# Sums of FFN weight blocks in a fused decoder block: from subtractions on VectorE to accumulating DMAs

## The chip, the cores and the metric

The kernel runs on one core of a Trainium2 chip. The metric is the device time of one execution in microseconds (us). The engines are TensorE (PE; PEld is its weight load), VectorE (DVE), ScalarE (ACT), GpSimd (POOL) and SyncE (SP). DMAs are issued from the queues of SP and POOL here and run on the core's 16 DMA engines.

## The reference

One decoder layer over 512 tokens and 2048 channels in float32: two attention branches, gated and merged, and a SwiGLU FFN of width 5632. What the change touches is the FFN:

```python
x = x + gt1 * (merged @ w_out)
h2 = _rms(x, g_norm2) * (1 + sc2) + sh2
gate, up = jnp.split(h2 @ w_ffn_in, 2, axis=-1)
x = x + gt2 * ((jax.nn.silu(gate) * up) @ w_ffn_out)
```

## The kernel before

The first half of the span holds the adaLN products, the two attention branches, the merge and `w_out`. Its weights come through another pool of tiles and are not touched.

Both FFN products are made as seven products of 2x2 blocks in place of eight (Winograd's form of Strassen's scheme): P1, P5, P7, P3, P6, P2, P4, in this order. Each multiplies a block of activations, or a sum of such blocks, with a block of weights, or a sum of such blocks. `BLOCK` names the four blocks of a weight 11, 12, 21 and 22. P1, P3 and P2 take the blocks 11, 22 and 21 as they are; P5, P7, P6 and P4 take sums, which build on one another in place (`INTO`, line 1173).

The work is a list of pieces, one per product and quarter (`j`) of the contraction. In the first matrix (FFN-in, `ffn_in_group`, line 1243) there are 11 groups of four column tiles with 7 x 4 = 28 pieces each. In the second (FFN-out, `ffn_out_chunk`, line 1418) a piece is one group of the contraction; the groups stand in chunks (`CH`, line 1395) of 3, 2, 2, 2 and 2, each done for two halves `q` of the output: 154 pieces. A piece's raw weights are a 128x1024 float32 tile (512 KB), in rows of 1 KB, or of 512 bytes in the first group. `raw_load` issues the load on SP's queue into a pool of ten such tiles. `piece_make` subtracts two raw tiles on DVE where the product asks for a sum, then splits the tile: ACT casts it to a float32r upper part `whi`, DVE subtracts that from the tile for the lower part `wlo`. There are three buffers of each part. PE then runs twelve matmuls of 512 columns per piece (`prod_mm`, line 1230).

The order is set by `ahead_to` (line 1209): before a piece's matmuls the pieces up to two ahead are made, and those up to six ahead are loaded. In this part DVE, ACT and POOL take the order that the framework's scheduler gives them; loads on SP stay in program order. On POOL's queue stand the parks: after each group of FFN-in 14 stores of 256 KB (`park`, line 1326, and one of `x`), which bring the activated blocks and their sums to DRAM. FFN-out reads them back as `yb` tiles by `y_load` on SP's queue. The activations' sums are made by `sums` (line 1087) and in `act_back2` (line 1347). `out_tiles` (line 1471) multiplies by the gate gt2 and stores the output.

Between the two halves of the program, `second_norms` (line 1384) applies the second norm and makes the activations' sums of eight pairs of tiles, while PE works on the first group's P5.

```python
    INTO = {"P5": "11", "P7": "12", "P6": "22", "P4": "21"}
    ...
            kd = (stage, g, INTO[prod], j)
            vec.tensor_tensor(raws[kd], raws[key], raws[stage, g, y, j], ALU.subtract)
            key = kd
```

Of the kernel before, what the change touches and what calls it, by code (L numbers as in the profile page):

```python
# [9 lines left out]
F32 = mybir.dt.float32  # L10
# [10 lines left out]
KD = D // P  # L21
# [66 lines left out]
def kernel(  # L88
# [50 lines left out]
    def ps(tag, w=T):  # L139
        return pp.tile([P, w], F32, tag=tag, name=nm("ps_" + tag), bufs=PSB[tag])  # L140
# [36 lines left out]
    def sync_dma(dst, src):  # L177
        tc.keep_in_program_order(nc.sync.dma_start(dst, src))
# [71 lines left out]
    for i in range(D // T):  # L250
# [118 lines left out]
    st = {}  # L369
# [41 lines left out]
    o = ps("y")  # L411
# [389 lines left out]
    for hh in range(H):  # L801
# [11 lines left out]
        src = mla_chunk(sw)  # L813
# [216 lines left out]

    def half_cols(th):
        return slice(th * 256, th * 256 + 256)

# [50 lines left out]

    def sums(a, b, put):

        lo, hi = slice(0, 256), slice(256, 512)
        s12, s34 = t2("s12"), t2("s34")  # L1090
        vec.tensor_tensor(s12[:, lo], a[:, hi], b[:, hi], ALU.add)
        vec.tensor_tensor(s12[:, hi], s12[:, lo], a[:, lo], ALU.subtract)
        put(1, split_t(s12, "x12"))
        vec.tensor_tensor(s34[:, lo], a[:, lo], a[:, hi], ALU.subtract)
        vec.tensor_tensor(s34[:, hi], b[:, lo], s12[:, hi], ALU.subtract)
# [38 lines left out]
    step(last_b, w_out_f[LM], 2048, 1024, 2048)  # L1134


    raws = {}
    BLOCK = {"11": (0, 0), "21": (1, 0), "12": (0, 1), "22": (1, 1)}

    def raw_src(key):  # L1140
# [12 lines left out]
    def raw_load(key):  # L1153
        if key in raws:
            return
        r = st["rp2"].tile([P, 1024], F32, tag="raw2", name=nm("raw2"))
        src, km = raw_src(key)
        sync_dma(r.rearrange("p (a b) -> p a b", b=128 if km else 256), src)
        raws[key] = r

    def kmc(key, ap):

# [2 lines left out]
        return ap.rearrange("p (m k c) -> p k m c", k=2, m=4)  # L1165


    PROD = {
        "P1": ((1, 1), "11", None), "P5": (1, "12", "11"), "P7": (3, "22", "12"), "P3": (4, "22", None),
        "P6": (2, "22", "11"), "P2": ((1, 2), "21", None), "P4": ((2, 2), "21", "22"),  # L1170
    }

    INTO = {"P5": "11", "P7": "12", "P6": "22", "P4": "21"}
    LAST = {"P7": ("12",), "P6": ("11",), "P4": ("21", "22")}

    def piece_keys(stage, g, prod, j):
        _, x, y = PROD[prod]
        return [(stage, g, b, j) for b in (y, x) if b]

    def piece_make(stage, g, prod, j):  # L1180
        _, x, y = PROD[prod]
        key = (stage, g, x, j)
        if y:
            kd = (stage, g, INTO[prod], j)
            vec.tensor_tensor(raws[kd], raws[key], raws[stage, g, y, j], ALU.subtract)
            key = kd
        r = raws[key]
        hi = wp.tile([P, 1024], F32R, tag="whi", name=nm("whi"), bufs=3)
        lo = wp.tile([P, 1024], F32R, tag="wlo", name=nm("wlo"), bufs=3)
        v4 = lambda t: t.rearrange("p (k m c) -> p k m c", k=2, m=4)  # L1190
        act.copy(v4(hi), kmc(key, r))
        vec.tensor_tensor(v4(lo), kmc(key, r), v4(hi).bitcast(F32), ALU.subtract)
        for b in LAST.get(prod, ()):
            del raws[stage, g, b, j]
        return hi, lo

    ev = []
    made = {}
    cur = {"load": 0, "make": 0}
    pieces = []  # L1200

    def add_piece(args, use):
# [4 lines left out]
        ev.append((None, fn))  # L1207

    def ahead_to(i, n_make, n_load):
        while cur["load"] < min(i + n_load + 1, len(pieces)) or cur["make"] < min(i + n_make + 1, len(pieces)):  # L1210
            if cur["load"] <= cur["make"] or cur["load"] < min(i + n_load + 1, len(pieces)):
                for key in piece_keys(*pieces[cur["load"]]):
                    raw_load(key)
                cur["load"] += 1
            else:
                made[cur["make"]] = piece_make(*pieces[cur["make"]])
                cur["make"] += 1

    def run_ev():
# [7 lines left out]
    def ffn_begin():  # L1227
        ahead_to(0, 0, 3)
# [14 lines left out]
    def ffn_in_group(g, order):  # L1243
# [86 lines left out]
    def back(src, j, o):  # L1330

        for b in range(2):
            for t in range(2):
                c = j + 2 * b
                pe.transpose(o[:, b * 256 + t * P:b * 256 + (t + 1) * P], src[t][:, c * P:(c + 1) * P], ident)

    def act_back1(g):
        src = [groups[g].pop(("a1", t)) for t in range(2)]
        for j in range(2):
            o = ps(("mm", "y")[j])  # L1340
            back(src, j, o)
            y = t2("y1")
            act.copy(y, o)
            park(2 * g + j, 0, split_t(y, "y1"))
            yraw[g, j] = y

    def act_back2(g):
        src = [groups[g].pop(("a2", t)) for t in range(2)]
        for j in range(2):
            o = ps(("mm", "y")[j])  # L1350
            back(src, j, o)
            y2 = t2("y2")
            act.copy(y2, o)
            y1 = yraw.pop((g, j))
            x = t2("x22", F32R)
            act.copy(x[:, 0:256], y2[:, 256:512])
            vec.tensor_tensor(x[:, 256:512], y2[:, 256:512], x[:, 0:256].bitcast(F32), ALU.subtract)
            nc.gpsimd.dma_start(apark[2 * g + j].rearrange("p (a x) -> p a x", x=T)[:, 2], x.bitcast(F32))

            lo, hi = slice(0, 256), slice(256, 512)  # L1360
            s12, s34 = t2("s12"), t2("s34")
            vec.tensor_tensor(s12[:, lo], y2[:, lo], y2[:, hi], ALU.add)
            vec.tensor_tensor(s12[:, hi], s12[:, lo], y1[:, lo], ALU.subtract)
            park(2 * g + j, 3, split_t(s12, "y12"))
            vec.tensor_tensor(s34[:, lo], y1[:, lo], y2[:, lo], ALU.subtract)
            vec.tensor_tensor(s34[:, hi], y1[:, hi], s12[:, hi], ALU.subtract)
            park(2 * g + j, 5, split_t(s34, "y34"))


# [101 lines left out]
    def out_tiles(q, col_):  # L1471
        xr_ = {}
        for i in range(4):
            m = 4 * (2 * q + col_) + i
            xr = t2("xo")
            sync_dma(xr, xpark[m])
            xr_[i] = xr
        for i in range(4):
            m = 4 * (2 * q + col_) + i
            o = ps(("mm", "y")[i % 2])  # L1480
            for r in range(2):
                for t in range(2):
# [110 lines left out]
```

## Time and profile before

| | us |
|---|---|
| three runs | 2691.06, 2693.76, 2694.64 |
| median | 2693.76 |
| the profiled execution | 2691.3 |
| its span, first to last instruction | 2689.6 |
| PE busy | 2584.3 |
| DVE busy | 2024.8 |
| ACT busy | 1149.4 |
| POOL busy | 154.9 |

The span is the time between the first and the last instruction of the profiled execution; 1.7 us of its own time lie around it. An engine's busy time is an average over stages with different limits, so the views below are taken by stage: from 1301 to 1391 us the second norm and the first sums, from 1400 to some 2236 FFN-in, then FFN-out, and the output's stores at the end. The mean granted clock of TensorE is 0.985 of full speed.

### The profile page before, as it was taken

How to read it: one execution, taken by the hardware profiler on the slowest of the kernel's cores; microseconds unless marked ns; L12 is line 12 of the kernel's file. 1: busy time of each engine (PE TensorE's matmuls, PEld its weight loads, DVE VectorE, ACT ScalarE, POOL GpSimd, SP SyncE). 2: the span in 40 equal slices, each digit the busy share in tenths (PEclk: the TensorE clock that was granted, in tenths of full speed). 3: DMA queues.
4: the chain of work that ended last, by engine and by line, in shares of the span. 5: the costliest groups of instructions: out<-in, count | busy, mean ns of one | idle time of the engine just before them, and what ended most of it. 6: DMA issues, size and time to landing. Idle time of an engine off the chain costs nothing.

```text
span 2689.6 us, 32101 instructions
## 1 busy us (share of the span) xinstructions
PE 2584.3 (96%) x12166; PEld 2147.2 (80%) x12166; DVE 2024.8 (75%) x2614; ACT 1149.4 (43%) x1557; POOL 154.9 (6%) x256
## 2 busy tenths in 40 slices
PE   6999999999999999999779999999999999999997
PEld 4788888888899888888558888888888887888885
DVE  8966766657877854533768888888888887689997
ACT  4434655542333322222545544455544445543331
POOL 0000000000110100000001100111110111000001
PEclk9999999999999999999879999999999999999998
DMA  9854444336666783332325445445444549765562
GB/s 341 300 195 164 160 150 143 128 134 235 252 248 251 263 347 141 141 141 98 94 63 167 144 136 160 158 144 172 151 136 151 164 135 327 235 210 193 189 206 79
DMA packets 236579, 487.29 MB, mean 181 GB/s; under 512 B 15428, under 2 KB 159044, under 8 KB 211336
## 3 DMA queue, kind: packets, MB, share of 16 engines
q1 hardware_dynamic: 215552, 426.03, 46.5%
q0 software_dynamic: 14816, 48.51, 5.0%
q10 hardware_dynamic: 6056, 10.70, 1.0%
q8 instruction: 95, 1.56, 0.2%
q14 instruction: 60, 0.49, 0.1%
HBM read 425.93 MB, written 59.24 MB: 180 GB/s over the span
## 4 chain that ended last, share of the span: by engine, by line
PE 71%; issue 17%; DVE 6%; DMA 3%; ACT 2%; POOL 0%; SPq 0%; POOLq 0%; ACTq 0%; DVEq 0%
PE ps_mm L82 48%; PE ps_s L82 11%; PE ps_t L82 8%; PE ps_y L82 5%; DMA raw<-in_w_ff_dram 2%; DVE wlo L82 2%; DVE raw L271 1%; ACT whi L82 1%; DVE s L82 0%; DVE raw L82 0%; DMA gpark<-sg 0%; DMA raw<-in_w_ada_dram 0%; POOL out_dram L1487 0%; DVE x L82 0%; DVE xr L82 0%
## 5 line engine op out<-in xcount | busy, mean ns | idle before, releaser
L82 ACT CAST whi<-raw 128x1024 fp32r<-128x1024 f32 x672 | 702.8, 1050 | 1037.7 <-PE ps_mm L82 471.6
L82 DVE TENSOR_TENSOR wlo<-raw,whi 128x1024 fp32r<-128x1024 f32 x672 | 815.7, 1218 | 341.2 <-ACT whi L82 338.5
L82 DVE TENSOR_TENSOR raw<-raw,raw 128x1024 f32<-128x1024 f32 x264 | 319.2, 1220 | 20.9 <-DMA raw<-in_w_ff_dram 17.7
L82 PE MATMUL ps_mm<-hl,whi 128*128 128x512 f32 x832 | 327.2, 393 | 0.0
L82 PE MATMUL ps_mm<-hh,whi 128*128 128x512 f32 x832 | 325.0, 391 | 0.0
L82 PE MATMUL ps_mm<-hh,wlo 128*128 128x512 f32 x832 | 324.9, 390 | 0.0
L271 DVE CUSTOM_DVE_ANT_0 raw<-raw,cb,cols 128x2048 f32<-128x2048 f32 x96 | 224.5, 2344 | 0.7 <-DMA raw<-in_w_ada_dram 0.7
L82 PE MATMUL ps_s<-whi,x 128*128 128x512 f32 x704 | 218.6, 392 | 0.1
L82 PEld LDWEIGHTS ps_mm<-hh,wlo 128*128 128x128 f32 x832 | 156.2, 188 | 32.7
L82 PEld LDWEIGHTS ps_mm<-hl,whi 128*128 128x128 f32 x832 | 156.6, 188 | 30.4
L82 PEld LDWEIGHTS ps_mm<-hh,whi 128*128 128x128 f32 x832 | 156.4, 188 | 30.5
L82 PEld LDWEIGHTS ps_s<-whi,x 128*128 128x128 f32 x704 | 133.3, 189 | 28.1 <-DVE x L82 0.6
L82 PE MATMUL ps_s<-wlo,x 128*128 128x512 f32 x352 | 139.3, 396 | 1.8 <-ACT x L82 1.8
L82 PE MATMUL ps_mm<-whi,yb 128*128 128x512 f32 x440 | 137.0, 393 | 0.0
L82 PE MATMUL ps_s<-whi,yb 128*128 128x512 f32 x352 | 108.5, 389 | 0.0
L82 PE MATMUL ps_t<-whi,yb 128*128 128x512 f32 x352 | 108.5, 389 | 0.0
L82 PE MATMUL ps_mm<-whi,x 128*128 128x512 f32 x352 | 108.4, 389 | 0.0
L82 PE MATMUL ps_t<-wlo,x12h 128*128 128x512 f32 x176 | 74.0, 421 | 30.5 <-ACT x12h L82 30.5
L82 PE MATMUL ps_mm<-mgl,whi 128*128 128x512 f32 (+1 forms) x272 | 102.7, 377 | 0.0
L82 PE MATMUL ps_mm<-mgh,whi 128*128 128x512 f32 (+1 forms) x272 | 102.4, 377 | 0.0
L82 PE MATMUL ps_mm<-mgh,wlo 128*128 128x512 f32 (+1 forms) x272 | 102.4, 377 | 0.0
L82 PEld LDWEIGHTS ps_mm<-whi,yb 128*128 128x128 f32 x440 | 83.5, 190 | 17.5
(363 smaller groups left out, 5147.6 us busy)
## 6 DMA issues: line engine op xcount, KB each, us to landing
raw<-in_w_ff_dram SPq DMA_DIRECT2D x264, 512.0 KB, 5.4
raw<-in_w_ada_dram SPq DMA_DIRECT2D x96, 1024.0 KB, 5.1
yb<-apark SPq DMA_DIRECT2D x154, 256.0 KB, 5.7
raw<-in_w_gate_dram SPq DMA_DIRECT2D x27, 1024.0 KB, 4.9
raw<-in_w_sb_dram SPq DMA_DIRECT2D x24, 1024.0 KB, 4.9
raw<-in_w_out_dram SPq DMA_DIRECT2D x16, 1024.0 KB, 4.8
raw<-in_w_gate_dram SPq DMA_DIRECT2D x24, 512.0 KB, 4.9
raw<-in_w_lat_dram SPq DMA_DIRECT2D x8, 1024.0 KB, 8.2
```

Source lines behind the costliest of these rows:

```text
L82: ins = f(*a, **kw)
L271: tc.keep_in_program_order(nc.vector.tensor_tensor_reduce(raw, raw, cb, 1.0, col(C_B + 16 * ADA[name] + j), ALU.mult, ALU.add, dst))
```

## The change

The signs of the scheme are moved, so that all four sums of weight blocks are plain sums: P5 takes 11 + 12, P7 takes 12 + 22, P6 takes 11 + 12 + 22 and P4 takes 11 + 12 + 22 + 21. The activations' sums change their signs to match, which makes half of their tensor_tensor instructions scalar_tensor_tensor with a factor of -1, and half of the output columns are multiplied by -gt2, which is made once by a new DVE instruction (`minus_gt2`).

The weights' sums are no longer made on DVE. A tile "a" is loaded with block 11 for P1. When P1's piece is made, a DMA on POOL's queue adds block 12 from DRAM to the same tile for P5; after P5's make another adds 22 for P6, and after P6's another adds 21 for P4. A tile "b" is loaded with 12, and a DMA adds 22 for P7. P3 and P2 load 22 and 21 as they are. So each of 66 sets of four blocks has four plain loads, as before, and four adding DMAs in place of four subtractions. `ahead_to` issues the add of P7 up to four pieces ahead of its make.

```diff
-    INTO = {"P5": "11", "P7": "12", "P6": "22", "P4": "21"}
-    LAST = {"P7": ("12",), "P6": ("11",), "P4": ("21", "22")}
 ...
+    PROD = {
+        "P1": ((1, 1), "a", "11", True), "P5": (1, "a", "+12", True), "P7": (3, "b", "12+22", False),
+        "P3": (4, "b", "22", False), "P6": (2, "a", "+22", True), "P2": ((1, 2), "b", "21", False),
+        "P4": ((2, 2), "a", "+21", False),
+    }
 ...
+    def raw_tile(key, r=None):
+
         src, km = raw_src(key)
-        sync_dma(r.rearrange("p (a b) -> p a b", b=128 if km else 256), src)
-        raws[key] = r
+        new = r is None
+        if new:
+            r = st["rp2"].tile([P, 1024], F32, tag="raw2", name=nm("raw2"))
+        dst = r.rearrange("p (a b) -> p a b", b=128 if km else 256)
+        if new:
+            sync_dma(dst, src)
+        else:
+            nc.gpsimd.dma_start(dst, src, accum_op=ALU.add)
+        return r
 ...
-    def piece_make(stage, g, prod, j):
-        _, x, y = PROD[prod]
-        key = (stage, g, x, j)
-        if y:
-            kd = (stage, g, INTO[prod], j)
-            vec.tensor_tensor(raws[kd], raws[key], raws[stage, g, y, j], ALU.subtract)
-            key = kd
-        r = raws[key]
+    def piece_make(i):
+        stage, g, prod, j = pieces[i]
+        _, tl, blk, keep = PROD[prod]
+        key = (stage, g, blk[-2:], j)
+        r = raws.pop(i)
 ...
         vec.tensor_tensor(v4(lo), kmc(key, r), v4(hi).bitcast(F32), ALU.subtract)
-        for b in LAST.get(prod, ()):
-            del raws[stage, g, b, j]
+        if keep:
+            n = next(n for n in range(i + 1, len(pieces))
+                     if pieces[n][:2] == (stage, g) and pieces[n][3] == j and PROD[pieces[n][2]][2][0] == "+")
+            raws[n] = r
+            piece_add(n)
         return hi, lo
 ...
             else:
-                made[cur["make"]] = piece_make(*pieces[cur["make"]])
+                while cur["add"] < min(cur["make"] + 4, cur["load"]):
+                    if "+" in PROD[pieces[cur["add"]][2]][2][1:]:
+                        piece_add(cur["add"])
+                    cur["add"] += 1
+                made[cur["make"]] = piece_make(cur["make"])
                 cur["make"] += 1
 ...
-            vec.tensor_tensor(s12[:, lo], y2[:, lo], y2[:, hi], ALU.add)
-            vec.tensor_tensor(s12[:, hi], s12[:, lo], y1[:, lo], ALU.subtract)
+            vec.tensor_tensor(s12[:, lo], y2[:, hi], y2[:, lo], ALU.subtract)
+            vec.scalar_tensor_tensor(s12[:, hi], s12[:, lo], -1.0, y1[:, lo], ALU.mult, ALU.subtract)
 ...
-            vec.scalar_tensor_tensor(xr, o, ada["gt2"][:, m:m + 1], xr, ALU.mult, ALU.add)
+            vec.scalar_tensor_tensor(xr, o, (ngt2 if col_ == 0 else ada["gt2"])[:, m:m + 1], xr, ALU.mult, ALU.add)
```

Three places show how the instructions move. The first is DVE in FFN-in's second group, around P3's end and P6; `raw` are the raw tiles, `wlo` and `whi` the parts. Before:

```order
L82 TENSOR_TENSOR raw_2047_11633<-raw_2047_11633,raw_2011_11445 128x1024
L82 TENSOR_TENSOR wlo_11879<-raw_2075_11735,whi_11878 128x1024
L82 TENSOR_TENSOR raw_2070_11714<-raw_2070_11714,raw_2016_11470 128x1024
L82 TENSOR_TENSOR raw_2075_11735<-raw_2075_11735,raw_2019_11489 128x1024
L82 TENSOR_TENSOR wlo_11898<-raw_2044_11614,whi_11897 128x1024
L82 TENSOR_TENSOR wlo_11917<-raw_2047_11633,whi_11916 128x1024
L82 TENSOR_TENSOR wlo_11936<-raw_2070_11714,whi_11935 128x1024
L82 TENSOR_TENSOR wlo_11957<-raw_2075_11735,whi_11956 128x1024
```

And now, at the same place:

```order
L82 TENSOR_TENSOR wlo_11869<-raw_2082_11796,whi_11868 128x1024
L82 TENSOR_TENSOR wlo_11885<-raw_2087_11816,whi_11884 128x1024
L82 TENSOR_TENSOR wlo_11903<-raw_2008_11432,whi_11902 128x1024
L82 TENSOR_TENSOR wlo_11922<-raw_2011_11450,whi_11921 128x1024
L82 TENSOR_TENSOR wlo_11941<-raw_2016_11474,whi_11940 128x1024
L82 TENSOR_TENSOR wlo_11962<-raw_2019_11492,whi_11961 128x1024
```

The subtractions of raw tiles are gone; DVE keeps one wlo a piece. In the whole program DVE has 2343 rows after 2606.

The second is POOL's queue at the boundary of FFN-in's second and third group, where the parks of y1 stand (`apark`). Before:

```order
L1328 DMA apark_317<-y1h_12175 128x2x256
L1328 DMA apark_317<-y1l_12176 128x2x256
L1328 DMA apark_318<-y1h_12188 128x2x256
L1328 DMA apark_318<-y1l_12189 128x2x256
L1358 DMA apark_317<-x_2168_12281 128x512
```

And now:

```order
L1169 DMA raw_2154_12230<-in_w_ff_dram 128x4x256
L1169 DMA raw_2157_12249<-in_w_ff_dram 128x4x256
L1169 DMA raw_2180_12331<-in_w_ff_dram 128x4x256
L1169 DMA raw_2185_12353<-in_w_ff_dram 128x4x256
L1169 DMA raw_2122_12050<-in_w_ff_dram 128x4x256
L1169 DMA raw_2125_12068<-in_w_ff_dram 128x4x256
L1169 DMA raw_2130_12092<-in_w_ff_dram 128x4x256
L1351 DMA apark_318<-y1h_12175 128x2x256
L1351 DMA apark_318<-y1l_12176 128x2x256
L1351 DMA apark_319<-y1h_12188 128x2x256
L1169 DMA raw_2133_12110<-in_w_ff_dram 128x4x256
L1351 DMA apark_319<-y1l_12189 128x2x256
```

The four adds of P7 (tiles 2154 to 2185) stand ahead of the four of P5 (tiles 2122 to 2133), though P5 comes first on PE, and three of the four parks ahead of P5's last add.

The third is POOL's queue in FFN-out. Before, nothing stood there between the last park and the output's stores:

```order
L1328 DMA apark_336<-y12h_17874 128x2x256
L1328 DMA apark_336<-y12l_17875 128x2x256
L1328 DMA apark_336<-y34h_17882 128x2x256
L1328 DMA apark_336<-y34l_17883 128x2x256
L1487 DMA out_dram<-xo_20838 128x512
```

Now it holds the adds; these are from the second chunk's end of the first half on:

```order
L1169 DMA raw_3386_18640<-in_w_ff_dram 128x4x256
L1169 DMA raw_3389_18658<-in_w_ff_dram 128x4x256
L1169 DMA raw_3452_19000<-in_w_ff_dram 128x4x256
L1169 DMA raw_3455_19019<-in_w_ff_dram 128x4x256
L1169 DMA raw_3386_18640<-in_w_ff_dram 128x4x256
L1169 DMA raw_3389_18658<-in_w_ff_dram 128x4x256
L1169 DMA raw_3440_18926<-in_w_ff_dram 128x4x256
L1169 DMA raw_3445_18946<-in_w_ff_dram 128x4x256
```

The tiles 3386 and 3389 are the first half's "a" tiles of two groups, with their second and third add; 3440 and 3445 are the next half's, with P5's add, and 3452 and 3455 its "b" tiles for P7. POOL has 525 rows after 260; SP's queue has 739 rows as before.

## Rows read from the trace of the kernel before

**Rows 1.** The page's first part: busy us (share of the span) and instructions by engine
```profile
PE 2584.3 (96%) x12166; PEld 2147.2 (80%) x12166; DVE 2024.8 (75%) x2614; ACT 1149.4 (43%) x1557; POOL 154.9 (6%) x256
```

**Rows 2.** Busy time by stretch: its length, the engines, PEclk, DMA share, GB/s
```profile
1300.00:1400.00 100.00, 62.40 (x222) 46.04 (x221) 81.28 (x152) 53.59 (x98) 0.54 (x1) 0.73 0.13 40
...
1400.00:2200.00 800.00, 788.32 (x3541) 649.24 (x3540) 671.67 (x742) 398.33 (x483) 96.74 (x140) 1.00 0.48 152
2256.00:2640.00 384.00, 380.87 (x1681) 314.36 (x1680) 327.35 (x333) 156.03 (x160) 4.35 (x8) 0.99 0.63 210
```

**Rows 3.** PE's waits: 1301 to 1391, 1400 to 2230, 2230 to 2300 us
```profile
PE ps_t L82 <- ACT x12h L82: 30.5, 7, 5.9
...
PE ps_mm L82 <- DVE wlo L82: 11.7, 10, 1.5
...
PE ps_mm L82 <- DVE wlo L82: 5.7, 1, 5.7
```

**Rows 4.** DVE's groups, 1301 to 1391 and 1400 to 2200 us: busy, mean ns
```profile
L82 DVE SCALAR_TENSOR_TENSOR xr<-xr,ada_gs,rstd 128x256 f32<-128x256 f32 x32 | 14.2, 477 | 0.1
L82 DVE TENSOR_TENSOR raw<-raw,raw 128x1024 f32<-128x1024 f32 x9 | 11.0, 1218 | 0.1
...
L82 DVE TENSOR_TENSOR s<-s,xr 128x256 f32<-128x256 f32 x8 | 3.4, 421 | 0.2
...
L82 DVE TENSOR_TENSOR wlo<-raw,whi 128x1024 fp32r<-128x1024 f32 x282 | 342.6, 1221 | 110.2 <-ACT whi L82 109.3
L82 DVE TENSOR_TENSOR raw<-raw,raw 128x1024 f32<-128x1024 f32 x160 | 192.6, 1219 | 19.0 <-DMA raw<-in_w_ff_dram 17.7
```

**Rows 5.** DMA, 1400 to 2200 us: queues (packets, MB, share), issues (KB, us to landing)
```profile
q1 hardware_dynamic: 84909, 84.32, 34.7%
q0 software_dynamic: 11200, 36.71, 12.8%
...
raw<-in_w_ff_dram SPq DMA_DIRECT2D x160, 512.0 KB, 5.8
```

**Rows 6.** DMA, 1424 to 1428 us: loads of raw tiles alone
```profile
DMA packets 1258, 1.26 MB, mean 314 GB/s; under 512 B 32, under 2 KB 1258, under 8 KB 1258
...
q1 hardware_dynamic: 1258, 1.26, 100.7%
```

**Rows 7.** DMA, 2400 to 2410 us: loads of raw and y tiles together
```profile
DMA packets 2857, 3.48 MB, mean 348 GB/s; under 512 B 146, under 2 KB 2171, under 8 KB 2857
...
q1 hardware_dynamic: 2857, 3.48, 100.5%
```

**Rows 8.** The parks' issues on POOL, 1400 to 2260 us: ns min/median/max, first, last
```profile
L1328 POOL DMA_DIRECT2D apark<-y1h x22: 707/707/715, 1438.3 to 2236.4; - x22
...
L1358 POOL DMA_DIRECT2D apark<-x x22: 552/552/555, 1450.5 to 2249.4; - x22
```

**Rows 9.** POOL in order of time: start, us; both y1h parks of one group
```profile
1518.48 0.71 POOL L1328 DMA_DIRECT2D apark<-y1h  x1 [53.40 <-ACT y1h L82]
...
1520.95 0.71 POOL L1328 DMA_DIRECT2D apark<-y1h  x1
```

**Rows 10.** SP's queue in order of time, FFN-out: the same loads one chunk apart
```profile
2342.37 31.01 SPq L178 DMA_DIRECT2D raw<-in_w_ff_dram  x8
...
2418.09 31.45 SPq L178 DMA_DIRECT2D raw<-in_w_ff_dram  x8
```

**Rows 11.** The raw tiles, 2300 to 2650 us: ns min/median/max; loads' landing in us
```profile
L82 ACT CAST whi<-raw x125: 1042/1054/1058, 2300.2 to 2647.0; 128x1024 fp32r<-128x1024 f32 x125
...
DMA to landing us min/median/max: 3.4/4.8/6.9
```

More of the change, by code (lines that the diff above doesn't have):

```diff
@@ L1071, with minus_gt2 @@
     X = {}
+    ngt2 = cp.tile([P, KD], F32, name="ngt2")
+    def minus_gt2():
+        vec.tensor_scalar(ngt2, ada["gt2"], -1.0, None, ALU.mult)
+    step(minus_gt2)
     def norm2(k, th):
@@ L1090, in sums @@
         s12, s34 = t2("s12"), t2("s34")
-        vec.tensor_tensor(s12[:, lo], a[:, hi], b[:, hi], ALU.add)
-        vec.tensor_tensor(s12[:, hi], s12[:, lo], a[:, lo], ALU.subtract)
+        vec.tensor_tensor(s12[:, lo], b[:, hi], a[:, hi], ALU.subtract)
+        vec.scalar_tensor_tensor(s12[:, hi], s12[:, lo], -1.0, a[:, lo], ALU.mult, ALU.subtract)
         put(1, split_t(s12, "x12"))
         vec.tensor_tensor(s34[:, lo], a[:, lo], a[:, hi], ALU.subtract)
-        vec.tensor_tensor(s34[:, hi], b[:, lo], s12[:, hi], ALU.subtract)
+        vec.scalar_tensor_tensor(s34[:, hi], b[:, lo], -1.0, s12[:, hi], ALU.mult, ALU.subtract)
         put(3, split_t(s34, "x34"))
@@ L1134 @@
     step(last_b, w_out_f[LM], 2048, 1024, 2048)
-    raws = {}
     BLOCK = {"11": (0, 0), "21": (1, 0), "12": (0, 1), "22": (1, 1)}
@@ L1151, in raw_src @@
         return src.rearrange("m p x -> p m x"), False
[L1153 to L1156, printed above, removed]
+    def raw_tile(key, r=None):
         src, km = raw_src(key)
-        sync_dma(r.rearrange("p (a b) -> p a b", b=128 if km else 256), src)
-        raws[key] = r
+        new = r is None
[7 more added lines that the diff above has]
+        return r
     def kmc(key, ap):
@@ L1168, with piece_load, piece_add @@
     PROD = {
-        "P1": ((1, 1), "11", None), "P5": (1, "12", "11"), "P7": (3, "22", "12"), "P3": (4, "22", None),
-        "P6": (2, "22", "11"), "P2": ((1, 2), "21", None), "P4": ((2, 2), "21", "22"),
-    }
-    INTO = {"P5": "11", "P7": "12", "P6": "22", "P4": "21"}
-    LAST = {"P7": ("12",), "P6": ("11",), "P4": ("21", "22")}
-    def piece_keys(stage, g, prod, j):
-        _, x, y = PROD[prod]
-        return [(stage, g, b, j) for b in (y, x) if b]
-    def piece_make(stage, g, prod, j):
-        _, x, y = PROD[prod]
-        key = (stage, g, x, j)
-        if y:
-            kd = (stage, g, INTO[prod], j)
-            vec.tensor_tensor(raws[kd], raws[key], raws[stage, g, y, j], ALU.subtract)
-            key = kd
-        r = raws[key]
+        "P1": ((1, 1), "a", "11", True), "P5": (1, "a", "+12", True), "P7": (3, "b", "12+22", False),
+        "P3": (4, "b", "22", False), "P6": (2, "a", "+22", True), "P2": ((1, 2), "b", "21", False),
+        "P4": ((2, 2), "a", "+21", False),
+    }
+    raws = {}
+    def piece_load(i):
+        stage, g, prod, j = pieces[i]
+        _, tl, blk, keep = PROD[prod]
+        if blk[0] != "+":
+            raws[i] = raw_tile((stage, g, blk[:2], j))
+    def piece_add(i):
+        stage, g, prod, j = pieces[i]
+        raw_tile((stage, g, PROD[prod][2][-2:], j), raws[i])
+    def piece_make(i):
+        stage, g, prod, j = pieces[i]
+        _, tl, blk, keep = PROD[prod]
+        key = (stage, g, blk[-2:], j)
+        r = raws.pop(i)
         hi = wp.tile([P, 1024], F32R, tag="whi", name=nm("whi"), bufs=3)
@@ L1198 @@
     made = {}
-    cur = {"load": 0, "make": 0}
+    cur = {"load": 0, "add": 0, "make": 0}
     pieces = []
@@ L1209, in ahead_to @@
     def ahead_to(i, n_make, n_load):
[L1210 to L1213, printed above, removed]
+        end = len(pieces)
+        while cur["load"] < min(i + n_load + 1, end) or cur["make"] < min(i + n_make + 1, end):
+            if cur["load"] < min(i + n_load + 1, end):
+                piece_load(cur["load"])
                 cur["load"] += 1
             else:
-                made[cur["make"]] = piece_make(*pieces[cur["make"]])
+                while cur["add"] < min(cur["make"] + 4, cur["load"]):
[3 more added lines that the diff above has]
+                made[cur["make"]] = piece_make(cur["make"])
                 cur["make"] += 1
@@ L1361, in act_back2 @@
             s12, s34 = t2("s12"), t2("s34")
-            vec.tensor_tensor(s12[:, lo], y2[:, lo], y2[:, hi], ALU.add)
-            vec.tensor_tensor(s12[:, hi], s12[:, lo], y1[:, lo], ALU.subtract)
+            vec.tensor_tensor(s12[:, lo], y2[:, hi], y2[:, lo], ALU.subtract)
+            vec.scalar_tensor_tensor(s12[:, hi], s12[:, lo], -1.0, y1[:, lo], ALU.mult, ALU.subtract)
             park(2 * g + j, 3, split_t(s12, "y12"))
             vec.tensor_tensor(s34[:, lo], y1[:, lo], y2[:, lo], ALU.subtract)
-            vec.tensor_tensor(s34[:, hi], y1[:, hi], s12[:, hi], ALU.subtract)
+            vec.scalar_tensor_tensor(s34[:, hi], y1[:, hi], -1.0, s12[:, hi], ALU.mult, ALU.subtract)
             park(2 * g + j, 5, split_t(s34, "y34"))
```

## The prediction

> **What bounds the kernel now.** First the busy times by engine [rows 1]: TensorE (PE) is busy for 2584 of 2690 us, VectorE (DVE) for 2025. Then the table by stage [rows 2], since that average mixes stages: from 1400 to 2200 us (the first FFN matrix, FFN-in) PE is busy for 788.3 of 800 us, from 2256 to 2640 (the second, FFN-out) for 380.9 of 384, and only between 1300 and 1400 has it gaps, 37.6 us. DVE has room in all of them, and the 16 DMA engines are half used in FFN-in (0.48) and 63% used in FFN-out. Third, what PE waits for [rows 3]: in 1301 to 1391 ScalarE's x12h, 30.5 us in 7 waits, behind a row of DVE work; in FFN-in ten waits of a group's lower weight part wlo, 11.7 us; 5.7 us once where FFN-out begins. That is all that a lighter DVE can give back: the FFN is bound by PE, and what the change takes from DVE is for the most part covered by matmuls.
>
> The step to which I hold each stage is how long PE takes. FFN-in: the first park of y1h stands at 1438.3, the last at 2236.4, 22 in 11 groups, and two of one group lie 2.5 us apart [rows 8, 9]: (2236.4 - 2.5 - 1438.3) / 10 = 79.6 us a group of 28 pieces. FFN-out: the same eight loads come at 2342.4 and at 2418.1 [rows 10], so 75.7 us a chunk of 28 pieces, 2.70 us a piece.
>
> **What goes.** 264 subtractions of two raw tiles leave DVE, 1.219 us each [rows 4]. In 1301 to 1391 there are 9, 11.0 us, in the chain that PE waits for. Against them stand 16 scalar_tensor_tensor of 128x256 (477 ns) where tensor_tensor took 421: 0.9 us. I take the difference, 10.1 us, as gained (0 if ScalarE's share of that chain is what ends last). The ten waits of FFN-in (11.7) and the one at 2254 (5.7) can go too. Together at most 27.5 us. The sign edits in FFN-in (four instructions a group, 56 ns more each) and the one multiplication of gt2 lie beside PE and cost nothing; DVE, at 672 of 800 us before, would cover them even with its old work. The last reads only another column.
>
> **What comes.** 264 accumulating DMAs of 512 KB on POOL's queue, beside 264 plain loads that stay on SP's. The bytes of weights moved in the FFN double. Three things can cost: POOL's issuing, the latency of one add, and the 16 DMA engines.
>
> POOL: a park of 128 rows takes 0.55 us to issue, one of 256 rows 0.71 [rows 8], so 512 rows about 1.03 by the same slope. 16 adds and 14 parks a group make some 26 us of 79.6: covered, also at twice that. In the queue the adds of P7 stand ahead of P5's, and a park between them; what a blocked add holds back is the next add.
>
> Latency: three buffers of hi and lo let a make start when PE begins the piece two before it. The make takes 1.05 + 1.22 us [rows 4, 11]. In FFN-out with two groups a chunk, P5 follows P1 by two pieces on the same tile, so from the end of P1's make to the last start of P5's there are 4 x 2.70 - 2 x 2.27 = 6.3 us; in FFN-in, at a distance of four pieces, 11.7. Issue and a plain 512 KB landing need 1.03 + 4.8 (at most 6.9) [rows 11]: 5.8 to 7.9 us. FFN-in is covered, FFN-out just.
>
> The DMA engines decide. A plain load at saturation: loads alone moved 314 GB/s with the engines at 100.7% [rows 6], 1.67 us per 512 KB. A park costs 36.71 MB over 140 in 12.8% of 800 us [rows 5], 0.73 us each, which is 358 GB/s, the software queue's own rate. Loads with y tiles reach 348 GB/s at 100.5% [rows 7]. An add is in no row. Below, it costs what a plain load does, 1.67. Above, if reading the weights, reading the tile and writing it overlap in nothing, 2 x 1.67 + 1.46 = 4.8. I take two passes at the software queue's rate, 2 x 1.46 = 2.93, because a sum has two operands to read and the queue with these rows of 1 KB is the nearest row. The page Collectives: The Full Stack of the Trainium skill (The bandwidth ceiling: the fold count and why AG ≠ RS ≠ AR) says that an add in the DMA path is slow for its two source reads on one ring, a measured ratio of 1.93 to a copy; no run here shows it. By that, as an estimate from the page, an add would be 1.93 x 1.67 = 3.2 us and the time 2886.
>
> **The sum.** FFN-in, per group: 16 loads 26.7, 14 parks 10.2, 16 adds 46.9, together 83.8 us against PE's 79.6: +4.2, ten times 42 us, and the 11.7 us of waits are not gained. FFN-out, per chunk of 28: 16 loads and 28 y tiles are 15.7 MB, 45.2 us at 348 GB/s, with 46.9 of adds 92.1 against 75.7: +16.4, 5.5 times 90 us, and the 5.7 at its start is not gained either. The first group's adds I cost at nothing: they fall into 1301 to 1391, where the DMA share of the stage is 0.13 [rows 2]. 42 + 90 - 10 = +122 on the profiled execution's 2691.3, that is 2813; the median of the runs stands 2.5 above it, less than 0.2%, or 5.4 us, which is about what a measurement of this kernel can tell from no change. SP's loads come later for it, since buffers come free later; late next is P5's make in FFN-out, and behind it PE.
>
> The price at which an add stays hidden follows: (79.6 - 36.9) / 16 = 2.67 us in FFN-in, (75.7 - 45.2) / 16 = 1.91 in FFN-out.
>
> **The rivals.**
> One pass: the second operand is read in the shadow of the load, and an add costs 1.67. FFN-in then fills 63.6 of 79.6 us, FFN-out 71.9 of 75.7. All 27.5 us are gained, 2663.8; at 95% use I allow 10 us of waits in FFN-out: 2674, faster. For it speaks that the engines' packets overlap reading and writing already; against it that two operands come through where one did. It decides below 1.9 us an add. Chance 0.27.
>
> Latency: adds are cheap in engine time but land late. At the longest landing of a plain load the add misses the 6.3 us by 1.6; eight half-chunks have two groups, 13 us: 2674 + 13 = 2687. It turns slower only over 10 us of issue and landing. Chance 0.08.
>
> Nothing overlaps: 4.8 us an add. FFN-in 36.9 + 76.8 = 113.7, +341; FFN-out 122, +255; 2691 + 596 - 10 = 3277. Chance 0.10.
>
> A price between the passes, 2.0 to 2.6: hidden in FFN-in, not in FFN-out, 2690 to 2740, most of it slower. Chance 0.06. That the change does nothing is left 0.02: the order shows the subtractions gone and the adds there.
>
> **The numbers.** Forecast 2813, chance 0.47, its own range 2740 (an add at 2.6, with the rest as it is) to 2914 (2 x 1.67: +10.7 and +22.9 a unit). PE's clock makes it no worse: it was 0.73 where PE was busy for 62 of 100 us [rows 2], a part of the time at the lower of its two levels, but where DMA bounds a stage PE has time. Faster: one pass and 0.01 of latency, 0.28. Within 0.2%: most of latency and the change that does nothing, 0.07. Slower: 0.47 + 0.10 + 0.06 + 0.02 = 0.65. The range, 2666 to 2950, takes in one pass without its best end and the forecast with some of the dearer prices; 3277 is outside.
>
> **What would show it.** The DMA share: near 1.0 in FFN-out and above 0.95 in FFN-in if the forecast holds; about 0.8 and 0.95 for one pass. The software queue's share and its bytes give the price of an add directly. PE's waits should name the cast or wlo behind a DMA on the raw tile, most in FFN-out, at P5 and P7; for latency they would stand at P5 alone, some 1.6 us each, with engines that have time left. DVE falls by some 320 us in every case. PE's waits for x12h falling from 30.5 to about 20 would bear out the 10 us. I am wrong if FFN-out's chunks still take 75.7 us with the DMA share below 0.9: then an add costs less than 1.9 us; or if a group of FFN-in takes over 100 us: then it costs more than two passes.

## The result, and the profile after

| | before | after |
|---|---|---|
| median of four runs, us | 2693.25 | 2877.81 |
| lowest and highest, us | 2691.06 to 2694.64 | 2872.18 to 2881.73 |
| the profiled execution, us | 2691.3 | 2877.05 |
| its span, us | 2689.6 | 2875.3 |

The changed kernel takes 1.0684 times as long (95% interval 1.0665 to 1.0704): it is slower by 184.6 us. The forecast was slower by 122, to 2813, with a range to 2950.

The page of the profile after, as [rows 1] and with the DMA slices, the two queues, the bytes read and the group of the adds' issues on POOL:

```profile
PE 2640.7 (92%) x12166; PEld 2176.6 (76%) x12166; DVE 1731.1 (60%) x2351; ACT 1142.0 (40%) x1557; POOL 495.1 (17%) x520
...
DMA  8845434357666933438899999999999999999995
...
q1 hardware_dynamic: 215552, 426.03, 43.4%
q0 software_dynamic: 162400, 186.94, 35.4%
...
HBM read 564.35 MB, written 59.24 MB: 217 GB/s over the span
...
L1169 POOL DMA_DIRECT2D raw<-in_w_ff_dram x264 | 341.0, 1386 | 968.4 <-DVE wlo L82 648.0
```

DVE lost 294 us of work (2024.8 to 1731.1) and the program became longer: DVE was not what bounded it. From the 19th of the 40 slices on, where the second norm and then the FFN begin, the row of the DMA engines is an unbroken row of eights and nines up to the last slice. Read the two queues against each other: the software queue moved 187 MB and took 35.4% of the engines' time, the hardware queue 426 MB for 43.4%.

By stage, as [rows 2]; FFN-out stands later now, so its stretch is another:

```profile
1300.00:1400.00 100.00, 69.57 (x259) 51.81 (x258) 71.45 (x145) 55.62 (x100) 20.94 (x16) 0.76 0.72 116
1400.00:2200.00 800.00, 731.36 (x3170) 596.19 (x3170) 444.78 (x523) 352.51 (x434) 276.59 (x271) 0.97 1.02 231
2420.00:2780.00 360.00, 304.74 (x1247) 244.15 (x1246) 177.73 (x193) 112.92 (x114) 68.75 (x57) 0.94 1.03 245
```

The last two columns hold the answer: the DMA share went from 0.48 to 1.02 in FFN-in and from 0.63 to 1.03 in FFN-out. The share adds up the times of the packets, so it can pass 1 where packets overlap. Engines that had room are full in the mean, and PE, which stood at 788 of 800 us, is at 731.

What PE waited for over the whole span, as [rows 3]:

```profile
PE ps_t L82 <- DVE wlo L82: 100.1, 43, 6.2
PE ps_mm L82 <- DVE wlo L82: 51.4, 13, 7.9
PE ps_t L82 <- ACT x12h L82: 23.1, 7, 6.2
```

The waits for x12h went from 30.5 to 23.1 us; the waits for wlo grew from 19.0 us over the whole span to 151. The name in the row is DVE's, but DVE is idle more than before. One step further back, in the chain of waits of FFN-out from 2509 to 2524 us (start, us, what):

```profile
2509.42 1.13 POOL raw L1169
2510.55 10.34 DMA raw<-in_w_ff_dram
...
2520.99 1.06 ACT whi L82
...
2522.07 1.24 DVE wlo L82
...
2523.35 0.74 PE ps_t L82 x2
```

An add lands after 10.34 us, then the cast (ACT) and the lower part (DVE) follow, then PE. Most of the time lies in the second row.

The DMA view of FFN-in, 1500 to 2200 us, as [rows 5]:

```profile
q0 software_dynamic: 75150, 95.11, 70.4%
q1 hardware_dynamic: 66622, 66.15, 30.9%
...
raw<-in_w_ff_dram SPq DMA_DIRECT2D x126, 512.0 KB, 5.5
raw<-in_w_ff_dram POOLq DMA_DIRECT2D x127, 512.0 KB, 10.5
apark<-y1h POOLq DMA_DIRECT2D x16, 256.0 KB, 13.8
...
apark<-y34h POOLq DMA_DIRECT2D x16, 256.0 KB, 10.1
```

**The price of an add** comes out of the first row: 70.4% of 700 us are 492.8 us of the 16 engines. 112 parks at 0.73 us take 82 of them; 411 us are left for 127 adds, 3.2 us each. The same working for the other runs below, per 512 KB, gives 3.1 to 3.4, and 2.9 in the one with P5 and P7, whose window cuts more adds off at its ends. It is a price in packet time, an estimate: the parks' 0.73 us is taken over from the kernel before. 126 loads on the other queue took 30.9% of 700, 1.72 us each.

By stage the loss divides so. Up to the first park of y1h: 1438.3 to 1432.6, -5.7 us. From there to its last park, which is ten groups of FFN-in: 798.1 to 882.8, +84.7. The rest: +106.7. One chunk of 28 pieces is 336 matmuls. At the rate of the row above, 1247 in 360 us, that is 97 us, and SP's rows of ten loads of raw tiles, one a chunk, begin at 2442.16, 2537.72 and 2640.30 us: 96 to 103 us a chunk, 99 in the mean, against 75.7 before [rows 10].

### The profile page after: what moved, and what is told of

The parts are those of the page before. It is cut to its first block, busy times and chain, and to the rows that moved or that the text cites. A ratio compares the mean times of both kernels' runs of the same rounds, so it can differ in the third digit from the quotient of the medians.

```text
span 2875.3 us, 32565 instructions
## 1 busy us (share of the span) xinstructions
PE 2640.7 (92%) x12166; PEld 2176.6 (76%) x12166; DVE 1731.1 (60%) x2351; ACT 1142.0 (40%) x1557; POOL 495.1 (17%) x520
## 3 DMA queue, kind: packets, MB, share of 16 engines
q1 hardware_dynamic: 215552, 426.03, 43.4%
q0 software_dynamic: 162400, 186.94, 35.4%
HBM read 564.35 MB, written 59.24 MB: 217 GB/s over the span
## 5 line engine op out<-in xcount | busy, mean ns | idle before, releaser
L1169 POOL DMA_DIRECT2D raw<-in_w_ff_dram x264 | 341.0, 1386 | 968.4 <-DVE wlo L82 648.0
L82 PEld LDWEIGHTS ps_mm<-hh,whi 128*128 128x128 f32 x832 | 156.5, 188 | 30.5
L867 POOL TENSOR_SCALAR_AFFINE_SELECT sa<-sa 128x128 f32<-128x128 f32 x32 | 17.3, 541 | 871.3 <-ACT sa L82 871.3
L82 PE MATMUL ps_mm<-whi,yb 128*128 128x512 f32 x440 | 146.3, 416 | 0.0
L82 PE MATMUL ps_mm<-wlo,yb 128*128 128x512 f32 x220 | 94.6, 430 | 53.6 <-DVE wlo L82 51.0
L82 PE MATMUL ps_t<-wlo,x34h 128*128 128x512 f32 x176 | 78.4, 446 | 43.3 <-DVE wlo L82 43.3
L82 PE MATMUL ps_t<-whi,yb 128*128 128x512 f32 x352 | 115.6, 411 | 0.0
L82 PEld LDWEIGHTS ps_mm<-whi,yb 128*128 128x128 f32 x440 | 90.4, 205 | 19.7
## 6 DMA issues: line engine op xcount, KB each, us to landing
raw<-in_w_ff_dram POOLq DMA_DIRECT2D x264, 512.0 KB, 10.5
```

The source lines that it names most:

```text
L82: ins = f(*a, **kw)
L867: nc.gpsimd.affine_select(a[:, dg], a[:, dg], pattern=[[-1, P]], compare_op=ALU.is_gt, fill=0.0, base=0, channel_multiplier=1)
L1169: nc.gpsimd.dma_start(dst, src, accum_op=ALU.add)
```

## The experiments

The theory: the adds' engine time fills the 16 DMA engines, and each stage lasts as long as the larger of PE's work and the DMA engines' work. Against it: the latency of an add, the order on POOL's queue, the cost of the new signs, or a plain second read of the weights.

**The signs alone.** The kernel before, with the new signs of the scheme; the sums stay on DVE.

```diff
-            vec.tensor_tensor(raws[kd], raws[key], raws[stage, g, y, j], ALU.subtract)
+            vec.tensor_tensor(raws[kd], raws[key], raws[stage, g, y, j], ALU.add)
```

> The signs alone are moved; the four sums of weight blocks stay on VectorE, as plain additions of two loaded tiles. My theory (the cost is in the DMA engines, the signs cost nothing): the time of the kernel before, 2693 us, within 0.2%. Rival (the scalar_tensor_tensor instructions and the new multiplication delay VectorE where TensorE waits for it): 2 to 6 us slower, between 1301 and 1391 us.

Measured: 2692.78 us, ratio 1.0002 (0.9992 to 1.0011). The edits of the signs cost nothing that ten runs can show.

**No sums at all.** The adds are left out, on DVE and on POOL.

```diff
-            nc.gpsimd.dma_start(dst, src, accum_op=ALU.add)
+            pass
```

> The sums of weight blocks are left out, on VectorE and as DMAs: P5, P6 and P4 use block 11 and P7 block 12 as they are. Nothing else changes against the changed kernel. This is the most that a lighter VectorE can give: my sum said 27.5 us, so 2664 to 2667 us. Rival (the gain was counted too high, since in the changed kernel the stage up to the first park of y1h became only 5.7 us shorter): 2675 to 2685 us.

Measured: 2664.48 us, ratio 0.9900 (0.9885 to 0.9915). 28 us is all that DVE's 264 sums were worth; the prediction had at most 27.5. The first park of y1h stands at 1433.0, in the changed kernel at 1432.6: the first group's adds cost nothing up to there.

**Plain copies in place of the adds.** Same queue, same order, same bytes from DRAM, but the tile is overwritten.

```diff
-            nc.gpsimd.dma_start(dst, src, accum_op=ALU.add)
+            nc.gpsimd.dma_start(dst, src)
```

> The same 264 DMAs on POOL's queue, in the same order, on the same tiles and with the same waits, as plain copies: the second block overwrites the first in place of being added to it. My theory (an add costs the engines two passes, 3.2 to 3.4 us against 1.5 to 1.7 for a copy): a group of FFN-in falls back to 78 to 80 us, a chunk of FFN-out to 76 to 79, in all 2665 to 2695 us. Rival (what costs is the wait itself: POOL's issue of 1.3 us, the queue's order and a landing between two makes of one tile): most of the loss stays, over 2790 us.

Measured: 2667.06 us, ratio 0.9907 (0.9891 to 0.9924): 211 us less than with the adds. Its FFN-in in the DMA view, 1500 to 2200 us:

```profile
q0 software_dynamic: 30672, 108.02, 47.1%
q1 hardware_dynamic: 76746, 77.41, 35.6%
...
raw<-in_w_ff_dram POOLq DMA_DIRECT2D x141, 512.0 KB, 5.6
```

141 copies and 126 parks: (0.471 x 700 - 92) / 141 = 1.69 us a copy, so an add costs 1.9 times as much. The software queue's packets differ too: 30672 here, for more bytes than the 75150 of the adds. And the second read of the weights, the doubled queue and POOL's issues are all here: none of them is the loss. What is lost is lost by the adding. The smaller packets are not it either: with the parks' packets taken off, an add's packet of 1 KB holds an engine for 411 x 16 / 66190 = 99 ns in the changed kernel, and one of SP's loads, which go in packets of 1 KB too, for 216.3 x 16 / 66622 = 52 ns.

**A quarter and three quarters of each add.** Every add takes only the first quarter, or the first three quarters, of a tile's columns. The diff is that of three quarters; `km` holds in the first group, where a tile has eight parts, and elsewhere it has four.

```diff
-            nc.gpsimd.dma_start(dst, src, accum_op=ALU.add)
+            q = 6 if km else 3
+            nc.gpsimd.dma_start(dst[:, 0:q], src[:, 0:q], accum_op=ALU.add)
```

> The same 264 accumulating DMAs in nearly the same order, each over a quarter of the columns (128 KB in place of 512), so that three quarters of each sum are left out. My theory (bytes through the engines): an add costs about 0.8 us of them, FFN-in and FFN-out are hidden, 2663 to 2680 us. Rival (an accumulating DMA has a latency that does not go with its bytes, and the makes wait for it): over 2750 us.

> The 264 accumulating DMAs over three quarters of the columns (384 KB); the last quarter of each sum is left out. My theory (an add costs 3.3 us of the engines per 512 KB, so 2.5 here, and a stage is lengthened by what does not fit beside TensorE): FFN-in 36.9 + 39.6 = 76.5 us of 78, hidden; FFN-out 45.2 + 39.6 = 84.8 us against 75.7, +9.1 a chunk, 5.5 times 50 us: about 2714 us, 2700 to 2735. Rival (the loss goes evenly with the bytes, from the quarter's 2664 to the whole add's 2878): about 2807 us.

Measured: 2664.01 us, ratio 0.9900 (0.9886 to 0.9915), and 2723.31 us, ratio 1.0114 (1.0100 to 1.0128). The quarter costs 0.83 us of engine time, (0.298 x 700 - 92) / 141, a fourth of the whole, and nothing of the program's time. The stages of three quarters:

```profile
1400.00:2200.00 800.00, 799.87 (x3607) 663.22 (x3606) 509.28 (x595) 403.50 (x491) 306.17 (x302) 1.00 0.99 237
```

FFN-in runs with the DMA engines at 0.99 and PE at 799.87 of 800, and not a microsecond is lost. The prediction's break-even was 2.67 us an add there; this one costs 2.5. FFN-out, with a break-even of 1.91, is beyond its own, and all of the loss is there: first to last park of y1h take 782.1 us, as with no sums (781.7). The loss in the program's time begins at a threshold in each stage; it does not go evenly with the bytes.

**Adds in FFN-in alone.** FFN-out's adds become plain copies.

```diff
+            if key[0] == "a":
+                nc.gpsimd.dma_start(dst, src, accum_op=ALU.add)
+            else:
+                nc.gpsimd.dma_start(dst, src)
```

> Accumulating DMAs in FFN-in, plain copies in their place in FFN-out (where the sums are therefore wrong). My theory: the stages lose apart from each other; FFN-in keeps its 88.1 us a group against 78.1 with copies, 10 us ten times, so 2667 + 100 = 2767 us (2755 to 2785), and FFN-out goes back to 76 us a chunk. Rival (one stage delays the other, or the price is set by the order of the queue in FFN-out): under 2730 or over 2800 us.

Measured: 2765.08 us, ratio 1.0269 (1.0255 to 1.0283). FFN-out's adds are then 2877.8 - 2765.1 = 113 us, FFN-in's 2765.1 - 2667.1 = 98. These two must add up to the whole; that the stages lose apart from each other is seen in their lengths. FFN-in takes 879.5 us from the first to the last park of y1h, 882.8 in the changed kernel; from there to the end it is 453.9 us, 453.6 with plain copies alone and 559.9 in the changed kernel.

**A mixture.** If a stage has room for some adds, a mixture should beat both kernels. The kernel before with plain sums, in which only P7's sum in FFN-in, or P5's and P7's, is made by a DMA and the others by DVE. The two differ in the list in the diff:

```diff
+    def by_dma(stage, prod):
+        return prod in {'a': ('P7',)}.get(stage, ())
 ...
+            if not by_dma(stage, prod):
+                vec.tensor_tensor(raws[kd], raws[key], raws[stage, g, y, j], ALU.add)
```

> As the mix of P5 and P7, but only P7's sum in FFN-in by accumulating DMA, four a group. Theory: 13.2 + 36.9 = 50.1 us of DMA; the ten waits at P7 (11.7 us) go, half of the gain between 1301 and 1391 us stays: 2675 to 2684 us. Rival (it is the number of VectorE's subtractions in FFN-in as a whole that counts): as the mix of both, within 3 us.

> All the work is done. In FFN-in the sums of P5 and P7 come by accumulating DMA and those of P6 and P4 on VectorE; in FFN-out all four are on VectorE. My theory: 8 adds a group, 26.4 + 36.9 = 63.3 us of DMA beside 78 of TensorE, hidden; VectorE is light enough where TensorE waited for it, between 1301 and 1391 us and at P7, so most of the 28 us that leaving the sums out gave is kept: 2667 to 2680 us, faster than both kernels. Rival (an add that lands late, after 10 us, delays P5): 2690 us or more.

Measured: with P7 alone **2676.57 us**, ratio 0.9938 (0.9926 to 0.9951), 16 us faster than the kernel before. With P5 and P7 2734.47 us, ratio 1.0155 (1.0141 to 1.0169): on the rival's side, 54 us or more beyond the theory. The DMA engines' mean share in FFN-in is only 0.74 with P5 and P7. ScalarE at the boundary of two groups (start, us, what, idle before and its releaser):

```profile
1605.36 0.62 ACT L82 CAST y1h<-y 128x512 fp32r<-128x512 f32 x1
1615.92 1.04 ACT L82 CAST whi<-raw 128x1024 fp32r<-128x1024 f32 x1 [9.94 <-DMA raw<-in_w_ff_dram]
```

The cast of P5's piece waits 9.94 us for its add. The median add lands after 13.9 us; P5's adds are behind P7's on POOL. Was it their order, P5's place, or the number of adds at the boundary? Four more runs.

**P5 ahead of P7.** The same, with the adds in the program's order.

```diff
-        nc.gpsimd.dma_start(dst, src, accum_op=ALU.add)
+        tc.keep_in_program_order(nc.gpsimd.dma_start(dst, src, accum_op=ALU.add))
```

> The kernel in which P5's and P7's sums of FFN-in are made by an accumulating DMA and the other sums by DVE (2734.5 us), its adds now held on POOL in the order in which the program writes them, so that P5's four adds of a group no longer stand behind P7's four. Its DMA demand in a group of FFN-in, 16 loads of 1.67 us, 8 adds of 3.3 and 14 parks of 0.73, is 63 us of some 78. Theory (the time was lost to the order on POOL's queue: an add that waits for a tile holds back adds and parks that could go): 2662 to 2690. Rival (eight adds with a landing of about 10 us come too close together at a group's boundary whatever their order): 2715 to 2740.

Measured: 2803.42 us, ratio 1.0417 (1.0400 to 1.0435). Both sides missed: it is worse by 69 us. The wait has moved to the product that now stands behind. PE's waits in 1440 to 2240 us:

```profile
PE ps_mm L82 <- DVE wlo L82: 97.1, 9, 12.4
```

ps_mm is P7's product here; once in each of nine groups PE waits for it, up to 12.4 us.

**The changed kernel's adds in program order**, by the same edit.

> The changed kernel with its 264 adds held on POOL in the order in which the program writes them; bytes and instructions as before. Theory (the loss is the adds' time on the 16 DMA engines, 3.3 us each, so the order matters little): 2850 to 2900. Rival (a good part of the loss is the order on POOL's queue, as it may be in the kernel that makes P5's and P7's sums by DMA): below 2830.

Measured: 3014.26 us, ratio 1.1197 (1.1180 to 1.1214), 136 us above the changed kernel; neither side had that. Its stages:

```profile
1400.00:2200.00 800.00, 647.52 (x2745) 523.52 (x2743) 389.85 (x454) 311.02 (x378) 243.24 (x238) 0.91 0.90 201
2420.00:2780.00 360.00, 306.17 (x1255) 245.25 (x1254) 167.62 (x179) 130.25 (x148) 80.15 (x72) 0.92 1.07 263
```

The second row stands as far behind the last park of FFN-in as that of the changed kernel does: 1235 matmuls against 1247. From the last park of y1h to the end it is 550 us, against 560. In FFN-out the order changes little. FFN-in runs 2745 matmuls against 3170, with the DMA engines at 0.90. What POOL and PE wait for from 1440 to 2240 us, and as the last row what POOL waited for in the changed kernel:

```profile
POOL raw L1169 <- DVE wlo L82: 386.7, 44, 29.4
PE ps_mm L82 <- DVE wlo L82: 154.6, 32, 13.3
...
POOL raw L1169 <- DVE wlo L82: 219.1, 53, 15.2
```

POOL's queue stands longer for a tile that is still to be read, up to 29.4 us at once, and PE waits for P7 (ps_mm), 0.3 us in the changed kernel. In the program's order P7's adds alternate with P6's, and each of those waits for P5's piece; that this is what makes P7's adds late is read off the code, not tested. So the order can cost FFN-in as much as the bytes do, 144 us (882.8 to 1027.0). How much of the changed kernel's own loss there a better order would give back is open, because its 1.02 is a mean as well. Two stretches of 10 us of the changed kernel, one within a group and one at a boundary:

```profile
1590.00:1600.00 10.00, 10.00 (x45) 8.29 (x45) 6.46 (x7) 4.69 (x6) 3.06 (x3) 1.00 0.66 204
...
1640.00:1650.00 10.00, 6.09 (x27) 4.70 (x25) 3.87 (x6) 4.18 (x6) 2.85 (x4) 0.92 1.09 349
```

PE is full in the first, where the DMA engines have room, and waits in the second, where they have none.

**P5 alone.**

```diff
-        return prod in {'a': ('P7',)}.get(stage, ())
+        return prod in {'a': ('P5',)}.get(stage, ())
```

> As the kernel in which P7's sum of FFN-in alone is made by an accumulating DMA (2676.6 us), but P5's sum instead of P7's: P5's add goes into the tile of P1 as soon as P1's piece is made. The DMA demand is the same, four adds in a group. Theory (four adds in a group fit, whichever product they serve, and their queue holds nothing back): 2668 to 2685, as for P7. Rival (latency: P5's add cannot start before P1's piece is made and P5's piece is wanted soon after, so its landing of about 10 us is waited for): 2690 to 2735.

Measured: 2735.81 us, ratio 1.0158 (1.0143 to 1.0173), on the rival's side, at the upper end of its range. But the add's latency is not the largest wait. DVE's waits in 1440 to 2240 us:

```profile
DVE raw L82 <- DMA raw<-in_w_ff_dram: 70.0, 37, 5.5
```

These are P7's sums, waiting for plain loads. With P5's sum off DVE, block 12 is first asked for by P7, in one step with 22, so two loads come where one came before. The run moved loads as well as adds, and does not isolate P5's place.

**P6 and P7.** Eight adds in a group again, but P6's add has two products of time.

```diff
+        if prod == "P5" and by_dma(stage, "P6"):
+            raw_add(stage, g, "P6", j)
```

> P6's and P7's sums of FFN-in by an accumulating DMA, P5's, P4's and all of FFN-out's by DVE: eight adds in a group of FFN-in, as in the kernel of P5 and P7 (2734.5 us), so the same DMA demand of 16 x 1.67 + 8 x 3.3 + 14 x 0.73 = 63 us of some 78. The difference is where the added sums stand: P6's add can start when P5's piece is made and its tile is wanted two products later, whereas P5's add stands between P1's piece and the very next product. Theory (what lost there is P5's place in the order, not the number of adds): 2664 to 2682. Rival (eight adds in a group are too many, by their landing and by POOL's queue): 2700 to 2740.

Measured: 2737.67 us, ratio 1.0162 (1.0146 to 1.0178). The theory fell, and the time lies in the rival's range: four more adds a group than with P7 alone, and 61 us. The trace shows where they go. Busy times in stretches of 10 us at the boundary of two groups:

```profile
1570.00:1580.00 10.00, 10.00 (x46) 8.28 (x45) 5.48 (x5) 3.78 (x4) 0.00 (x0) 1.00 0.00 0
...
1610.00:1620.00 10.00, 10.00 (x49) 8.34 (x48) 7.42 (x9) 5.71 (x8) 7.43 (x8) 1.00 1.11 234
1620.00:1630.00 10.00, 10.00 (x46) 8.26 (x45) 7.78 (x11) 5.35 (x8) 5.92 (x8) 1.00 1.21 228
1630.00:1640.00 10.00, 8.32 (x37) 6.57 (x35) 3.19 (x5) 3.13 (x5) 2.85 (x4) 1.00 1.09 323
1640.00:1650.00 10.00, 7.51 (x22) 5.98 (x23) 5.60 (x6) 4.12 (x5) 0.00 (x0) 0.66 0.91 297
```

The mean of 0.73 hides that the DMA engines stand still from 1570 us and are full from 1610 to 1640, when most of the eight adds, the 14 parks and the next loads come together. The parks share the software queue with the adds; those of y34h land after 10.9 us (median), 3.7 before. DVE and ScalarE in the same stretch:

```profile
1637.76 0.69 DVE L82 TENSOR_TENSOR y34l<-s,y34h 128x512 fp32r<-128x512 f32 x1 [4.22 <-DMA apark<-y34h]
...
1638.56 0.58 ACT L82 COPY z<-ps_t 128x512 f32<-128x512 f32 x1 [5.43 <-DMA apark<-y34l]
```

Both wait until a park has left the buffer that they write next; the casts and lower parts of the next pieces are queued behind them. PE waits for a lower part 39.5 us in nine groups from 1440 to 2240, and after the wait the granted clock of the stretch is 0.66, a part of it at the lower of the two levels (1.2 and 2.4 GHz): 22 matmuls in 7.51 us, where full stretches have 46 in 10. The slower matmuls are most of the rest: from 1400 to 2200 us PE takes 759.72 us for 3320, with P7 alone 800.00 for 3609, 229 ns each against 222, some 24 us. In the kernel with P7 alone, four adds in this place, DVE waits for no park and z for parks of x only, 6.0 us in nine waits (here 45.8). Whether it is the number of adds or their meeting with the parks, no run separates. In the changed kernel both waits are there, from 1440 to 2300 us:

```profile
ACT whi L82 <- DMA raw<-in_w_ff_dram: 120.1, 36, 7.0
ACT z L82 <- DMA apark<-y34l: 45.7, 9, 6.4
...
DVE y34l L82 <- DMA apark<-y34h: 32.5, 9, 3.8
```

FFN-in's length, from the first to the last park of y1h, beside the DMA engines' mean share from 1400 to 2200 us:

| kernel | us | share |
|---|---|---|
| before | 798.1 | 0.48 |
| no sums | 781.7 | 0.48 |
| plain copies | 781.7 | 0.83 |
| a quarter of each add | 781.8 | 0.66 |
| three quarters of each add | 782.1 | 0.99 |
| the change | 882.8 | 1.02 |
| adds in FFN-in alone | 879.5 | 1.03 |
| P7 by DMA | 782.5 | 0.64 |
| P5 by DMA | 844.1 | 0.60 |
| P6, P7 by DMA | 846.4 | 0.73 |
| P5, P7 by DMA | 850.3 | 0.74 |
| P5, P7, program order | 914.4 | 0.71 |
| the change, program order | 1027.0 | 0.90 |

A high share alone costs nothing up to 0.99 in these runs; a low one is no safety when the adds stand together. Whether eight adds a group that are spread over it would fit was not tried.

## Why the prediction was right, and where it was off

**What bounds the kernel: right.** PE bound the FFN and DVE's sums were covered. With no sums at all the gain is 28 us, forecast at most 27.5. The parts were off: up to the first park 5.3 us in place of 10.1, since x12h still waits 23.1 us behind ScalarE and what remains of DVE's chain (ScalarE's share was named as the bound of that gain); FFN-in 16.4 in place of 11.7; the rest 3.8 in place of 5.7.

**What decides: right.** In the mean the 16 DMA engines were full in both stages, as the prediction said one would see (near 1.0 in FFN-out, above 0.95 in FFN-in). A plain copy of the same bytes hides, so an add costs more than the copy's 1.69 us. The two break-evens were borne out from both sides: 2.5 us an add fits FFN-in (2.67) and not FFN-out (1.91).

**The term that was mis-sized** is the price of an add: two passes at the software queue's rate, 2 x 1.46 = 2.93 us. It measured 3.2 in FFN-in and, by the same working in 2420 to 2780 us, 0.533 x 360 / 57 = 3.4 in FFN-out. It is as much as two passes, but two of a load of weights, 1.67 [rows 6] or 1.69 as a copy on POOL's queue, and not two of a park; that the engines read the two operands one after the other, no run shows directly. The prediction chose the park's rate because it was that of the same queue, with rows of 1 KB; but the parks went in packets of 3.3 KB in the mean (36.71 MB in 11200 [rows 5]), the adds in packets of 1 KB. The nearest row was the load of the same blocks, and 2 x 1.67 stood as the upper end of the forecast's own range. Why a copy of weights costs more than a park of as many bytes, 1.69 against 1.46, is not settled: on this queue their packets are about as large. With 3.2 and 3.4 the prediction's own sums give a group of FFN-in 36.9 + 16 x 3.2 = 88.1 us and a chunk of FFN-out 45.2 + 16 x 3.4 = 99.6. Measured: (882.8 - 2.0) / 10 = 88.1, and 99. That agreement is in part no test, since these prices come from the DMA share of the same stages. With the price from runs whose engines had room, 4 x 0.83 = 3.3 for the quarter and (0.305 x 700 - 92) / 36 = 3.4 with P7 alone, the sums give 89.7 to 91.3 and 98.0 to 99.6, still within 1 to 3 us. FFN-out as a whole lost 106.7 us and not 5.5 x (99.6 - 75.7) = 131: the sum takes every chunk as bound by the DMA engines from end to end, and in the last one, for one, they were not full (share 0.67 from 2800 to 2850 us). A small error in the price was a large one in the time, because only what stands above the threshold counts: 0.3 us more on 2.93 turned +42 us in FFN-in into +85.

The page Collectives: The Full Stack of the Trainium skill (The bandwidth ceiling: the fold count and why AG ≠ RS ≠ AR) says that the add of a reduce-scatter is slow because it needs two source reads, both on one ring, and gives 1.93 as the measured ratio of an all-gather's rate, which copies, to a reduce-scatter's. For an add from DRAM into a tile these runs agree in the ratio: 3.2 to 3.4 against 1.69 is 1.9 to 2.0, and the estimate of 2886 worked out from that page is nearer to 2877.8 than the forecast.

**The first group's adds at nothing: right.** The first park stands at 1432.6 with them and at 1433.0 without any sum, though the DMA share between 1300 and 1400 us went from 0.13 to 0.72.

**POOL's issue covered: right, but mis-sized.** An add's issue takes 1.39 us in the mean, not 1.03; POOL is busy for 277 of 800 us.

**Signs cost nothing: right.** 1.0002.

**The rivals.** One pass fell by the software queue's share, and so did nothing overlaps (4.8 us). Latency as such is not what the changed kernel lost by: plain copies in the same order, with the same waits between the makes, lose nothing, and the kernel's engines are full in the mean. But an add's landing is waited for, and the prediction looked for it in the wrong place. It took the landing of a plain load (4.8 to 6.9 us) for that of an add; adds land after 7.0 us (median) with four in a group, 10.5 in the changed kernel's FFN-in and 13.9 with P5's and P7's behind each other. And it looked at P5 in FFN-out, where the runs with fewer adds show it at the boundary of two groups of FFN-in. The prediction saw a park between the adds on POOL's queue, but put the order at nothing, where the program's order cost 136 us more; that DVE and ScalarE wait for the parks to free their buffers was not in it at all.

## What to carry to other kernels

A sum moved from an engine to an accumulating DMA is not free work: count it as two copies of its bytes on the 16 DMA engines, per stage, and compare with what the stage has left; here that came within 3 us of a group of FFN-in and of a full chunk of FFN-out, and 25 us above the whole loss of FFN-out. The gain was capped beforehand by how little the relieved engine had bound. Below the threshold, look at where the adds stand and what shares their queue: eight adds that met fourteen parks lengthened FFN-in by 64 us against four adds (846.4 to 782.5), at a mean share of 0.73 of the DMA engines.

## What the runs showed of the hardware

- An accumulating DMA of 512 KB into a tile took 3.2 to 3.4 us of the 16 DMA engines, a plain copy on the same queue 1.69. It is proportional to the bytes: 0.83 us for a quarter, (0.640 x 700 - 92) / 142 = 2.5 for three quarters.
- The adds go in packets of 1 KB, the rows of the weights: without the parks' 80 each [rows 5], (75150 - 112 x 80) / 127 = 521 an add. Plain copies of the same blocks on the same queue go in (30672 - 126 x 80) / 141 = 146 packets each, and cost no less than SP's loads in rows of 1 KB.
- The bytes read from HBM rose by 138 MB (425.93 to 564.35), which is 264 times 512 KB: a read of the tile itself is not among them.
- POOL took 1.29 us (median) to issue an add of 512 rows, where a park of 256 rows took 0.71 before.
